# Products of the MLPs' downward weights taken in pairs, by seven block products of half the size

## The chip, the cores and the metric

The kernel runs on one core of a Trainium2 chip. The metric is device time in microseconds (us) of one execution, median of several.

## The reference, cut to what matters

One step of a trunk of two layers on 544 columns (512 new tokens and 8 x 4 sampled ones), width 1024. Each layer is a token mixer (SSD in the first, HGRN in the second) and an MLP, which is what the change is in:

```
h = h + out.astype(h.dtype)
h = h + squared_relu_mlp(rmsnorm(h, norm_mlp_w[layer]), mlp_w_up[layer], mlp_w_down[layer]).astype(h.dtype)
...
def squared_relu_mlp(u, w_up, w_down):
    return jnp.square(jax.nn.relu(u @ w_up)) @ w_down
```

`w_up` is 1024 x 4096, `w_down` 4096 x 1024. All is f32; both a weight and an operand are split into a high and a low part, and a product is taken as high x high, high x low and low x high.

## The kernel before

**Units.** Weights arrive by SyncE's queue in units of 128 x 1024 f32 (`raw`, three buffers). A unit has eight blocks of 128 x 128. `split` (L192, L193) makes the high half on ScalarE (a cast, `whi` or `fh`) and the low half on VectorE (a subtraction, `wlo` or `fl`), for 512 columns at a time. A direct product of a unit (`products`, matmul at L320) is 8 blocks x 3 x 2 halves of 272 columns = 48 matmuls into one PSUM tile of two banks (`acc`).

**Groups.** Each MLP has four groups, q=0 to 3, of 8 units upward and 8 downward. The units of the first MLP are 56 to 119, so q=1 has the ups 72 to 79 and the downs 80 to 87. An up unit gives 128 rows of the hidden layer, which are squared and split into `gh` and `gl` (`g_tiles`, L1012); a down unit multiplies the eight `g` of its group, and the sum is added to the residual `x` (`add_to_x`, L410, 544 columns).

**Pairs.** The ups of q=1 to 3 are taken two at a time by a scheme of seven products. The pair of units and the operand make 2 x 2 blocks, and seven products p1, p2, n6, q7, n5, p3, q4 of sums of blocks take the place of eight: `seventh` (matmul at L1038, 12 matmuls each). The sums of the weights come by DMA and VectorE: `v` is loaded in two halves by SyncE's queue, and GpSimd's queue then adds two more to it in flight; `s2` is one sum, rebuilt in place between n6 and q7 (L245, L249); `a22` is the last block. The sums of the operand are made once per MLP (`operands`). The products share three banks (a, b of `pp`, and `pc`), and between them values are copied out: `s1` after p1, `sv` after n6, `sw` after n5 (L1047, ScalarE); VectorE adds or subtracts them (L1051, L1053, L1055), ScalarE does the relu (L1057, L1059, L1063).

**What sets the order.** `_mlp_plan` writes the list of products: in the pairs by the slots

```
SLOTS = (("p1", 0), ("p2", 1), ("n6", 3), ("q7", 4), ("n5", 6), ("p3", 9), ("q4", 12))
```

at 7 i + t for pair i, so that p3 and q4 of a pair stand among the next pair's products. The first two downs of a group are cut in pieces around the last products of its pairs, and the last down of a group around the first products of the next. `take` makes the weight halves ahead of a product (`conv_unit`, `form`), and loads ahead of these (`load_next`). A scheduler then sets the order of each engine's queue; what stands under `tc.high_priority()` goes forward in it. Each engine runs its queue in order. Halves of sevenths have rings of five of their own, `v` has three buffers, `s2` and `a22` two.

**The ends.** In the last group of each MLP, `then` follows an add to x (`pre_norm`: a scaled split and squares for the next norm). The last two downs of the second MLP are computed by `finish` together with the final norm.

Of the kernel before, what the change touches and what calls it, by code (L numbers as in the profile page):

```python
# [16 lines left out]
P = 128  # L17
# [43 lines left out]
def _mlp_plan(ub):  # L61


    plan = []
    for q in range(MLP_GROUPS):
        b = ub + 16 * q
        if q == 0:
            plan += [("u", b + i) for i in range(8)]
        else:
            slots = sorted((7 * i + t, name, b + 2 * i) for i in range(4) for name, t in SLOTS)  # L70
            slots = [x[1:] for x in slots]
            last = plan.pop()
            piece = lambda k0, k1: last[:2] + (k0, k1) + last[4:]
            plan += [piece(0, 4)] + slots[:2] + [piece(4, 6)] + slots[2:4] + [piece(6, 8)] + slots[4:]
        downs = [("d", b + 8 + m, 0, 8, m, q) for m in range(KT)]
        if q:
            cut = lambda x, k0, k1: x[:2] + (k0, k1) + x[4:]
            tail = plan[-2:]
            plan[-2:] = [cut(downs[0], 0, 4), tail[0], cut(downs[0], 4, 6), tail[1], cut(downs[1], 0, 6), cut(downs[0], 6, 8), cut(downs[1], 6, 8)]
            downs = downs[2:]  # L80
        plan += downs
    return plan
# [14 lines left out]
def trunk(ctx: ExitStack, tc: tile.TileContext, io):  # L97
# [44 lines left out]
    def plan_mlp(ub):  # L142
        plan = _mlp_plan(ub)
        for x in plan:
            if x[0] in "ud":
                if x[0] == "u" or x[2] == 0:
                    loads.append(("u", x[1]))
                    jobs.append((("u", x[1]), len(loads) - 1))
            else:
                if x[0] == "p1":  # L150
                    loads.extend([("v", x[1]), ("u", x[1])])
                if x[0] == "q4":
                    loads.append(("a22", x[1]))
                jobs.append((x, len(loads) - 1))
        return plan

    plans = [plan_mlp(U_MLP)]
# [3 lines left out]
    plans.append(plan_mlp(U_MLP2))  # L161
# [4 lines left out]
    def load_next():  # L166
        kind, u = loads[state["load"]]
        state["load"] += 1
        if kind == "u":
            raw = wraw.tile([P, 1024], F32, tag="raw", name=f"raw{u}")  # L170
            nc.sync.dma_start(raw, io["W"][u])
        elif kind == "a22":
            raw = mp["w"].tile([P, 512], F32, tag="a22", bufs=2, name=f"a22_{u}")
            nc.sync.dma_start(raw, io["W"][u + 1][:, 512:])
        else:

            raw = mp["w"].tile([P, 1024], F32, tag="v", bufs=3, name=f"v{u}")
# [61 lines left out]
    def form(name, u):  # L239
# [3 lines left out]
        if name == "n6":  # L243
            s2 = mp["w"].tile([P, 512], F32, tag="s2", bufs=2, name=f"s2_{u}")
# [708 lines left out]
    def mlp(name, plan, v0, then, last=False):  # L953
        es = ExitStack()
        pool = es.enter_context(tc.tile_pool(name=f"{name}_pool", bufs=4, reuse_waits="tile"))
        gp = es.enter_context(tc.tile_pool(name=f"{name}_g", bufs=9, reuse_waits="tile"))
        ws = es.enter_context(ExitStack())
        mp["w"] = ws.enter_context(tc.tile_pool(name=f"{name}_w", bufs=2, reuse_waits="tile"))
        res = []
        fops = {}  # L960

        sums = []

        def operands():
# [4 lines left out]
            for k in range(4):  # L969
# [14 lines left out]
                t12, t34 = (mp["w"].tile([P, T], F32, tag=f"f{c}", bufs=5, name=f"{name}_t{c}{k}") for c in "hl")  # L984
# [39 lines left out]

        def seventh(name_, u):

            if name_ == "p1":
# [7 lines left out]
            for k in range(4):  # L1035
                oh, ol = fops[name_, k]
# [5 lines left out]
            tick()  # L1042
            keep = {"p1": "s1", "n6": "sv", "n5": "sw"}.get(name_)
            with tc.high_priority():
                if keep:
                    d[keep] = pool.tile([P, HF], F32, tag=keep, bufs=1 + (keep == "sv"), name=f"{keep}_{u}")
                    nc.scalar.copy(d[keep], ps)  # L1047
                if name_ in ("p1", "n6"):
# [20 lines left out]
        for x_ in plan:  # L1069
            if x_[0] == "u":  # L1070
                held.append((x_[1], up(x_[1])))
                if len(held) == 2 or res:
# [6 lines left out]
            elif x_[0] == "d":  # L1079
                _, u, k0, k1, m, q = x_  # L1080
                if k0 == 0:
# [399 lines left out]
def _layout(inp):  # L1481
# [38 lines left out]
    units += mlp(1)  # L1520
# [58 lines left out]
```

## Time and profile before

| | |
|---|---|
| median of 3 runs | 1560.85 us (1560.81 to 1562.58) |
| the profiled execution | 1563.88 us |
| its span | 1562.1 us |
| mean granted TensorE clock | 0.992 |
| matmuls | 13420 |
| first MLP, second MLP | about 465 to 840 us and 1171 to 1548 us |

The span is the profiled part of that execution; a row is read as time, duration, engine, line and tiles, where a tile's buffer numbers are left out (`fh_p` is the high half of the weights of p1, p2 or p3, `fh_n` of n5 or n6, `fh_q` of q4 or q7). PE is TensorE's matmuls, PEld its weight loads, DVE VectorE, ACT ScalarE, POOL GpSimd, SP SyncE.

### The profile page before, as it was taken

How to read it: one execution, taken by the hardware profiler on the slowest of the kernel's cores; microseconds unless marked ns; L12 is line 12 of the kernel's file. 1: busy time of each engine (PE TensorE's matmuls, PEld its weight loads, DVE VectorE, ACT ScalarE, POOL GpSimd, SP SyncE). 2: the span in 40 equal slices, each digit the busy share in tenths (PEclk: the TensorE clock that was granted, in tenths of full speed). 3: DMA queues.
4: the chain of work that ended last, by engine and by line, in shares of the span. 5: the costliest groups of instructions: out<-in, count | busy, mean ns of one | idle time of the engine just before them, and what ended most of it. 6: DMA issues, size and time to landing. Idle time of an engine off the chain costs nothing.

```text
span 1562.1 us, 32717 instructions
## 1 busy us (share of the span) xinstructions
PE 1540.7 (99%) x13420; PEld 1478.1 (95%) x13420; DVE 1092.5 (70%) x2142; ACT 769.4 (49%) x1506; POOL 119.9 (8%) x195
## 2 busy tenths in 40 slices
PE   8999999999999999999999999999999999999997
PEld 7998989898999999999999999999999999999996
DVE  7889798969778555464655788888877555474544
ACT  5684757666355445273654333333344446273552
POOL 3211111110010000010000000000001001010001
PEclk9999999999999999999999999999999999999998
DMA  6466556473545245363323223333235245363311
GB/s 193 111 189 174 144 157 184 110 227 103 149 120 144 88 122 150 95 176 108 84 68 108 78 84 86 109 97 98 74 109 161 89 121 142 108 172 97 97 55 58
DMA packets 87926, 188.94 MB, mean 121 GB/s; under 512 B 14496, under 2 KB 34880, under 8 KB 87776
## 3 DMA queue, kind: packets, MB, share of 16 engines
q1 hardware_dynamic: 74704, 164.21, 33.4%
q0 software_dynamic: 11808, 21.50, 8.7%
q8 instruction: 105, 1.72, 0.4%
q10 hardware_dynamic: 1264, 1.14, 0.2%
q14 instruction: 45, 0.37, 0.1%
HBM read 169.64 MB, written 17.18 MB: 120 GB/s over the span
## 4 chain that ended last, share of the span: by engine, by line
PE 95%; DVE 2%; DMA 1%; issue 1%; ACT 0%; POOL 0%; SPq 0%; POOLq 0%; ACTq 0%
PE ps L320 28%; PE pd L320 24%; PE pp L1038 11%; PE po L320 6%; PE pm L320 6%; PE pc L1038 5%; PE pho L320 3%; PE pa L1177 1%; PE py L624 1%; PE pu L615 1%; PE pi L636 1%; DMA raw<-in_W 1%; PE pn L767 1%; PE pS L1280 1%; PE po L1303 1%
## 5 line engine op out<-in xcount | busy, mean ns | idle before, releaser
L192 ACT CAST whi<-raw 128x512 fp32r<-128x512 f32 x318 | 195.3, 619 | 402.1 <-PE ps L320 156.2
L193 DVE TENSOR_TENSOR wlo<-raw,whi 128x512 fp32r<-128x512 f32 x318 | 218.2, 688 | 94.1 <-ACT whi L192 92.1
L320 PE MATMUL pd<-gh,whi 128*128 128x272 f32 x992 | 205.9, 288 | 0.0
L320 PE MATMUL pd<-gl,whi 128*128 128x272 f32 x992 | 205.4, 288 | 0.0
L320 PE MATMUL pd<-gh,wlo 128*128 128x272 f32 x992 | 205.1, 288 | 0.0
L320 PEld LDWEIGHTS pd<-gh,whi 128*128 128x128 f32 x992 | 156.0, 188 | 0.0
L320 PEld LDWEIGHTS pd<-gh,wlo 128*128 128x128 f32 x992 | 155.7, 188 | 0.0
L320 PEld LDWEIGHTS pd<-gl,whi 128*128 128x128 f32 x992 | 155.5, 188 | 0.0
L320 PE MATMUL ps<-uh_s,whi 128*128 128x272 f32 x576 | 125.6, 300 | 2.5 <-DVE BC L501 2.4
L320 PE MATMUL ps<-ul_s,whi 128*128 128x272 f32 x576 | 121.1, 292 | 0.0
L320 PE MATMUL ps<-uh,whi 128*128 128x272 f32 x512 | 112.7, 300 | 0.0
L320 PE MATMUL ps<-ul,whi 128*128 128x272 f32 x512 | 106.5, 289 | 0.0
L320 PE MATMUL ps<-uh,wlo 128*128 128x272 f32 x512 | 106.2, 289 | 0.0
L410 DVE TENSOR_TENSOR x<-pd,x 128x544 f32<-128x544 f32 x62 | 44.8, 722 | 86.9 <-PE pd L320 86.9
L320 PEld LDWEIGHTS ps<-uh_s,whi 128*128 128x128 f32 x576 | 91.9, 192 | 8.5 <-issue 6.9
L320 PEld LDWEIGHTS ps<-ul_s,whi 128*128 128x128 f32 x576 | 92.0, 191 | 0.3
L181 POOL DMA_DIRECT2D v<-in_W x48 | 42.1, 1028 | 603.8 <-DMA v<-in_W 397.4
L320 PE MATMUL ps<-uh_s,wlo 128*128 128x272 f32 x576 | 85.7, 289 | 0.0
L320 PEld LDWEIGHTS ps<-uh,whi 128*128 128x128 f32 x512 | 80.8, 189 | 3.7 <-issue 1.4
L320 PEld LDWEIGHTS ps<-ul,whi 128*128 128x128 f32 x512 | 80.4, 188 | 0.0
L320 PEld LDWEIGHTS ps<-uh,wlo 128*128 128x128 f32 x512 | 80.1, 188 | 0.0
L320 PEld LDWEIGHTS ps<-uh_s,wlo 128*128 128x128 f32 x576 | 77.4, 188 | 1.1 <-issue 0.8
(428 smaller groups left out, 3811.4 us busy)
## 6 DMA issues: line engine op xcount, KB each, us to landing
raw<-in_W SPq DMA_DIRECT2D x198, 512.0 KB, 3.6
v<-in_W SPq DMA_DIRECT2D x48, 256.0 KB, 4.2
v<-in_W POOLq DMA_DIRECT2D x48, 256.0 KB, 5.8
wlo<-in_W POOLq DMA_DIRECT2D x34, 256.0 KB, 5.7
w<-cum_d SPq DMA_DIRECT2D x16, 512.0 KB, 6.9
st<-in_ssm_in SPq DMA_DIRECT2D x16, 512.0 KB, 4.9
out_ssm_s<-st SPq DMA_DIRECT2D x16, 512.0 KB, 6.8
a<-in_W SPq DMA_DIRECT2D x24, 256.0 KB, 4.3
```

The costliest lines, as they stand in the source:

```text
L181: nc.gpsimd.dma_start(raw[:, c : c + 512], io["W"][u + 1][:, :512], accum_op=ADD)
L192: nc.scalar.copy(hi, raw)
L193: (eng or nc.vector).tensor_tensor(lo, raw, hi.bitcast(F32), SUB)
L320: nc.tensor.matmul(ps[:, h, :HF], block(a, c0 + k * step), o[:, h * HF : (h + 1) * HF], start=(first and i == 0), stop=(last and i == len( ...
L410: nc.vector.tensor_tensor(v3(x[m]), ps[:, :, :HF], v3(x[m]), ADD)
L615: nc.tensor.matmul(pu, bt[:, c], xts[c].rearrange("p h q -> p (h q)"), start=True, stop=True)
L624: nc.tensor.matmul(py[64 * (h % 2) : 64 * (h % 2) + 64, (h // 2) * P : (h // 2 + 1) * P], xds[c][:, h], ws_[c][:, h], start=True, stop=True,)
L636: nc.tensor.matmul(pi[:, j * P : (j + 1) * P], hT[:, j * P : (j + 1) * P], CT[:, cs], start=True, stop=True)
L767: nc.tensor.matmul(pn, bm[:, s], xq.rearrange("p h q -> p (h q)"), start=True, stop=True)
L1038: nc.tensor.matmul(ps, block(w, k * P), o, start=(name_ in ("p1", "p2", "q7") and k == 0 and j == 0), stop=(k == 3 and j == 2), skip_group ...
L1177: nc.tensor.matmul(pv4[b * NS : (b + 1) * NS, c], K[:, bs], QQ[:, 2 - n :, bs], start=True, stop=True, tile_position=(0, b * NS),)
L1280: nc.tensor.matmul(pS[:, c * P : (c + 1) * P], kt[:, c], vt[:, c], start=True, stop=True)
```

## The change

The downs m=2 to 7 of the groups q=1, 2 and 3 are taken by the seven products too, as three pairs a group; in the last group of the second MLP it is m=2 to 5, and m=6 and 7 stay with `finish`. The pairs of downs of a group stand in one list of slots with the next group's pairs of ups. m=0 and m=1 stay direct, cut in pieces as before. For these pairs, sums of the squares' blocks are needed: `square_forms` makes them for each pair of ups with four instructions of 272 columns in the place of the squares themselves (L1052 to L1055) and splits them (two more high and low halves of 544 columns, `m0_gh72_0` and the like). A product of a pair of downs goes into x by itself: three copies (`s1`, `sv`, `sw`, now L1091) and seven adds of 272 columns (L1097 from a copy, L1100 from PSUM) in place of two of 544 (now L424). To make room, `v` goes to two buffers, `s2` and `a22` to one, `g` to eight, and the halves of sevenths share the ring of four of the direct units (`whi`, `wlo`), counted by `state["live"]`. The host lays the columns of these downs out in pairs.

```diff
 MLP_GROUPS = 4
-def _mlp_plan(ub):
+def _mlp_plan(ub, last):
     plan = []
+    pairs = []
+    part = lambda x, k0, k1: x[:2] + (k0, k1) + x[4:]
+    def slots():
+        found = sorted((7 * i + t, name, u) for i, u in enumerate(pairs) for name, t in SLOTS)
+        return [x[1:] for x in found]
     for q in range(MLP_GROUPS):
         b = ub + 16 * q
+        downs = [("d", b + 8 + m, 0, 8, m, q) for m in range(KT)]
         if q == 0:
-            plan += [("u", b + i) for i in range(8)]
-        else:
-            slots = sorted((7 * i + t, name, b + 2 * i) for i in range(4) for name, t in SLOTS)
-            slots = [x[1:] for x in slots]
-            last = plan.pop()
-            piece = lambda k0, k1: last[:2] + (k0, k1) + last[4:]
-            plan += [piece(0, 4)] + slots[:2] + [piece(4, 6)] + slots[2:4] + [piece(6, 8)] + slots[4:]
-        downs = [("d", b + 8 + m, 0, 8, m, q) for m in range(KT)]
-        if q:
-            cut = lambda x, k0, k1: x[:2] + (k0, k1) + x[4:]
-            tail = plan[-2:]
-            plan[-2:] = [cut(downs[0], 0, 4), tail[0], cut(downs[0], 4, 6), tail[1], cut(downs[1], 0, 6), cut(downs[0], 6, 8), cut(downs[1], 6, 8)]
-            downs = downs[2:]
-        plan += downs
+            plan += [("u", b + i) for i in range(8)] + downs
+            continue
+        pairs += [b + 2 * i for i in range(4)]
+        new = slots()
+        if q == 1:
+            d = plan.pop()
+            new = [part(d, 0, 4)] + new[:2] + [part(d, 4, 6)] + new[2:4] + [part(d, 6, 8)] + new[4:]
+        plan += new[:-2] + [part(downs[0], 0, 4), new[-2], part(downs[0], 4, 6), new[-1]]
+        plan += [part(downs[1], 0, 6), part(downs[0], 6, 8), part(downs[1], 6, 8)]
+        whole = last and q == MLP_GROUPS - 1
+        pairs = [b + 8 + m for m in range(2, KT - 2 if whole else KT, 2)]
+        if q == MLP_GROUPS - 1:
+            plan += slots() + (downs[-2:] if whole else [])
     return plan
...
-            raw = mp["w"].tile([P, 512], F32, tag="a22", bufs=2, name=f"a22_{u}")
+            raw = mp["w"].tile([P, 512], F32, tag="a22", bufs=1, name=f"a22_{u}")
             nc.sync.dma_start(raw, io["W"][u + 1][:, 512:])
         else:
-            raw = mp["w"].tile([P, 1024], F32, tag="v", bufs=3, name=f"v{u}")
+            raw = mp["w"].tile([P, 1024], F32, tag="v", bufs=2, name=f"v{u}")
...
         a1 = loaded["u", u]
         v = loaded.get(("v", u))
         if name == "n6":
-            s2 = mp["w"].tile([P, 512], F32, tag="s2", bufs=2, name=f"s2_{u}")
+            s2 = mp["w"].tile([P, 512], F32, tag="s2", bufs=1, name=f"s2_{u}")
             nc.vector.tensor_tensor(s2, v[:, :512], a1[:, :512], ADD)
             loaded["s2", u] = s2
...
             "p1": lambda: a1[:, :512], "p2": lambda: a1[:, 512:], "n6": lambda: s2, "q7": lambda: v[:, 512:],
             "n5": lambda: v[:, :512], "p3": lambda: loaded["s2", u], "q4": lambda: loaded["a22", u],
         }[name]()
-        hi = mp["w"].tile([P, 512], F32R, tag="fh", bufs=5, name=f"fh{u}_{name}")
-        lo = mp["w"].tile([P, 512], F32R, tag="fl", bufs=5, name=f"fl{u}_{name}")
+        hi = wcv.tile([P, 512], F32R, tag="whi", name=f"fh{u}_{name}")
+        lo = wcv.tile([P, 512], F32R, tag="wlo", name=f"fl{u}_{name}")
         split(raw, hi, lo)
         return [hi], [lo]
+    def halves_of(job):
+        return 2 if job[0][0] == "u" else 1
+    def ahead():
+        while state["conv"] < len(jobs) and state["live"] + halves_of(jobs[state["conv"]]) <= 4:
+            state["live"] += halves_of(jobs[state["conv"]])
+            conv_unit()
     def take(key):
         i = place[key]
-        ahead = 0.0
-        j = i
-        while j + 1 < len(jobs) and ahead < 1.0:
-            j += 1
-            ahead += 1.0 if jobs[j][0][0] == "u" else 0.25
-        while state["conv"] <= j:
-            if jobs[state["conv"]][0][0] != "u" and not mp:
-                break
-            conv_unit()
+        if mp:
+            ahead()
+            assert state["conv"] > i
+        else:
+            while state["conv"] <= min(i + 1, len(jobs) - 1) and jobs[state["conv"]][0][0] == "u":
+                conv_unit()
         return ready.pop(key)
     def unit(u):
...
     def mlp(name, plan, v0, then, last=False):
         es = ExitStack()
         pool = es.enter_context(tc.tile_pool(name=f"{name}_pool", bufs=4, reuse_waits="tile"))
-        gp = es.enter_context(tc.tile_pool(name=f"{name}_g", bufs=9, reuse_waits="tile"))
+        gp = es.enter_context(tc.tile_pool(name=f"{name}_g", bufs=8, reuse_waits="tile"))
         ws = es.enter_context(ExitStack())
+        tp = ws.enter_context(tc.tile_pool(name=f"{name}_t", bufs=8, reuse_waits="tile"))
         mp["w"] = ws.enter_context(tc.tile_pool(name=f"{name}_w", bufs=2, reuse_waits="tile"))
+        state["live"] = 2 * len(ready)
         res = []
         fops = {}
+        gops = {}
+        first = plan[0][1]
         sums = []
...
-                t12, t34 = (mp["w"].tile([P, T], F32, tag=f"f{c}", bufs=5, name=f"{name}_t{c}{k}") for c in "hl")
+                t12, t34 = (tp.tile([P, T], F32, tag=f"t{c}", name=f"{name}_t{c}{k}") for c in "hl")
...
         banks = {}
+        def square_forms(u, a0, a1):
+            k = (u - first) % 16 // 2
+            (h0, l0), (h1, l1) = g[u], g[u + 1]
+            gops["p1", k] = h0[:, :HF], l0[:, :HF]
+            gops["p2", k] = h1[:, :HF], l1[:, :HF]
+            gops["p3", k] = h1[:, HF:], l1[:, HF:]
+            b11, b12, b21, b22 = a0[:, :HF], a0[:, HF:], a1[:, :HF], a1[:, HF:]
+            nc.vector.tensor_tensor(b11, b11, b12, SUB)
+            nc.vector.tensor_tensor(b12, b12, b22, SUB)
+            nc.vector.scalar_tensor_tensor(b22, b11, -1.0, b22, MUL, SUB)
+            nc.vector.tensor_tensor(b21, b21, b22, ADD)
+            for i, (t, n1, n2) in enumerate(((a1, "q4", "n6"), (a0, "n5", "q7"))):
+                th, tl = (tp.tile([P, T], F32R, tag=f"t{c}", name=f"{name}_g{c}{u}_{i}") for c in "hl")
+                split(t, th, tl)
+                gops[n1, k] = th[:, :HF], tl[:, :HF]
+                gops[n2, k] = th[:, HF:], tl[:, HF:]
+        def release(n):
+            state["live"] -= n
         def seventh(name_, u):
+            q, r = divmod(u - first, 16)
+            down = r >= 8
+            ops_ = gops if down else fops
             if name_ == "p1":
                 ac = acc_tile(f"pp{u}")
                 banks[u] = d = {"a": ac[:, 0, :HF], "b": ac[:, 1, :HF]}
...
             ps = d[{"p2": "b", "q7": "c", "q4": "c"}.get(name_, "a")]
             hi, lo = take((name_, u))
             for k in range(4):
-                oh, ol = fops[name_, k]
+                oh, ol = ops_[name_, k]
                 for j, (w, o) in enumerate(((hi, oh), (hi, ol), (lo, oh))):
                     nc.tensor.matmul(
                         ps, block(w, k * P), o, start=(name_ in ("p1", "p2", "q7") and k == 0 and j == 0),
                         stop=(k == 3 and j == 2), skip_group_check=name_ in ("n6", "n5", "p3", "q4"),
                     )
             tick()
+            release(1)
             keep = {"p1": "s1", "n6": "sv", "n5": "sw"}.get(name_)
-            with tc.high_priority():
-                if keep:
+            if keep:
+                with tc.high_priority():
                     d[keep] = pool.tile([P, HF], F32, tag=keep, bufs=1 + (keep == "sv"), name=f"{keep}_{u}")
                     nc.scalar.copy(d[keep], ps)
+            if down:
+                m = r - 8
+                x1, x2 = ([x[i][:, :HF], x[i][:, HF:]] for i in (m, m + 1))
+                at = {"p1": x1[0], "p2": x1[0], "p3": x1[1], "n6": x2[0], "q4": x2[0], "n5": x2[1], "q7": x2[1]}[name_]
+                if keep:
+                    nc.vector.tensor_tensor(at, at, d[keep], ADD if name_ == "p1" else SUB)
+                else:
+                    with tc.high_priority():
+                        nc.vector.tensor_tensor(at, ps, at, ADD)
+                if q == MLP_GROUPS - 1 and name_ in ("p3", "q4"):
+                    then(m + (name_ == "q4"))
+                return
+            with tc.high_priority():
                 if name_ in ("p1", "n6"):
                     d[name_] = pool.tile([P, T], F32, tag="a", name=f"a{u}_{name_}")
                 if name_ == "p2":
...
             if name_ == "q4":
                 nc.scalar.activation(d["n6"], d["n6"], AF.Relu)
                 g_tiles(u + 1, d["n6"])
+                square_forms(u, d["p1"], d["n6"])
         g = {}
         acc = {}
...
         for x_ in plan:
             if x_[0] == "u":
                 held.append((x_[1], up(x_[1])))
+                release(2)
                 if len(held) == 2 or res:
                     if not res:
                         while not res:
...
                         finish([unit(u - 1), unit(u)], ops, [acc[KT - 2][0], acc[m][0]])
                         continue
                     acc[m][1] = unit(u)
+                else:
+                    ahead()
                 ps, w = acc[m]
                 gb = u - 8 - m
                 products(ps, w, [g[gb + k] for k in range(k0, k1)], k0 == 0, k1 == 8, k0 * P)
+                release((k0 < 4 <= k1) + (k1 == 8))
                 if k1 == 8:
                     add_to_x(m, ps, then if q == MLP_GROUPS - 1 else None)
             else:
...
-    def mlp(l):
+    def mlp(l, last):
...
+            ms = slice(2, 2 if q == 0 else KT - 2 if last and q == MLP_GROUPS - 1 else KT)
+            d[ms] = d[ms].reshape(-1, P, KT // 2, 2, P).transpose(0, 1, 3, 2, 4).reshape(-1, P, 1024)
...
```

Three places in the queues, each in the first MLP's second group (q=1). A name's last number is the tile's own; `gh`, `gl` are halves of squares, `a` the squares and before them the values, `m0_g...` the halves of the sums of squares.

ScalarE, around the copy `sv_76` of the third pair, before:

```order
L192 CAST fh76_n5_7165<-v76_6867 128x512
L192 CAST fh78_p1_7191<-raw78_7042 128x512
L1057 ACTIVATE a74_p1_6994<-pp74_6974 128x272
L1059 ACTIVATE a76_p1_7144<-a76_p1_7144 128x272
L1012 ACTIVATE a74_p1_6994<-a74_p1_6994 128x544
L1047 COPY sv_76_7207<-pp76_7124 128x272
L192 CAST gh74_7183<-a74_p1_6994 128x544
L192 CAST fh78_p2_7211<-raw78_7042 128x512
L192 CAST fh76_p3_7227<-s2_76_7103 128x512
```

and after:

```order
L200 CAST fh76_n5_7198<-v76_6912 128x512
L200 CAST gh74_7194<-a74_p1_6992 128x544
L1116 ACTIVATE a76_p1_7154<-a76_p1_7154 128x272
L200 CAST fh78_p1_7222<-raw78_7061 128x512
L200 CAST fh78_p2_7238<-raw78_7061 128x512
L1091 COPY sv_76_7214<-pp76_7133 128x272
L200 CAST fh76_p3_7273<-s2_76_7134 128x512
L1120 ACTIVATE a74_n6_7054<-a74_n6_7054 128x544
L1030 ACTIVATE a74_n6_7054<-a74_n6_7054 128x544
L1091 COPY sw_76_7289<-pp76_7133 128x272
```

`gh74` and the cast `fh78_p2` of the next pair's second product stood behind `sv_76`; now they stand ahead of it.

VectorE, from the low half `fl76_n6` of the third pair to `gl74`, before:

```order
L193 TENSOR_TENSOR fl76_n6_7106<-s2_76_7103,fh76_n6_7105 128x512
L245 TENSOR_TENSOR s2_78_7250<-v78_7037,raw78_7042 128x512
L249 TENSOR_TENSOR s2_76_7103<-s2_76_7103,raw76_6872 128x512
L1053 TENSOR_TENSOR a74_n6_7062<-pc74_7063,sw_74_7121 128x272
L193 TENSOR_TENSOR fl76_q7_7127<-v76_6867,fh76_q7_7126 128x512
L193 TENSOR_TENSOR gl73_7100<-a72_n6_6922,gh73_7099 128x544
L193 TENSOR_TENSOR wlo81_1_7422<-raw81_7292,whi81_1_7420 128x512
L193 TENSOR_TENSOR fl74_q4_7148<-a22_74_6995,fh74_q4_7147 128x512
L1051 TENSOR_TENSOR a76_p1_7144<-pp76_7124,s1_76_7142 128x272
L193 TENSOR_TENSOR fl76_n5_7166<-v76_6867,fh76_n5_7165 128x512
L193 TENSOR_TENSOR fl78_p1_7192<-raw78_7042,fh78_p1_7191 128x512
L193 TENSOR_TENSOR gl74_7184<-a74_p1_6994,gh74_7183 128x544
```

and after:

```order
L201 TENSOR_TENSOR fl76_n6_7137<-s2_76_7134,fh76_n6_7136 128x512
L1054 SCALAR_TENSOR_TENSOR a72_n6_6910<-a72_p1_6860,a72_n6_6910 128x272
L257 TENSOR_TENSOR s2_76_7134<-s2_76_7134,raw76_6917 128x512
L1055 TENSOR_TENSOR a72_n6_6910<-a72_n6_6910 128x272
L201 TENSOR_TENSOR fl76_q7_7157<-v76_6912,fh76_q7_7156 128x512
L201 TENSOR_TENSOR fl74_q4_7177<-a22_74_7012,fh74_q4_7176 128x512
L201 TENSOR_TENSOR m0_gl72_0_7107<-a72_n6_6910,m0_gh72_0_7106 128x544
L201 TENSOR_TENSOR m0_gl72_1_7111<-a72_p1_6860,m0_gh72_1_7110 128x544
L1108 TENSOR_TENSOR a76_p1_7154<-pp76_7133,s1_76_7152 128x272
L201 TENSOR_TENSOR fl76_n5_7199<-v76_6912,fh76_n5_7198 128x512
L201 TENSOR_TENSOR gl74_7195<-a74_p1_6992,gh74_7194 128x544
L1052 TENSOR_TENSOR a74_p1_6992<-a74_p1_6992 128x272
```

The last two forms of pair 72, two low halves of its sums (`m0_gl72_0`, `m0_gl72_1`) and the first form of pair 74 have come in; the sum `s2_78` and the low half of direct unit 81 have gone to a later place.

VectorE at the first downs of the group behind the direct ones, before:

```order
L193 TENSOR_TENSOR gl79_7497<-a78_n6_7358,gh79_7496 128x544
L193 TENSOR_TENSOR wlo82_1_7506<-raw82_7334,whi82_1_7504 128x512
L410 TENSOR_TENSOR x_75<-pd1_0_7406,x_75 128x544
L193 TENSOR_TENSOR wlo83_0_7578<-raw83_7411,whi83_0_7576 128x512
L410 TENSOR_TENSOR x_75<-pd1_1_7500,x_75 128x544
L193 TENSOR_TENSOR wlo83_1_7579<-raw83_7411,whi83_1_7577 128x512
L193 TENSOR_TENSOR wlo84_0_7638<-raw84_7417,whi84_0_7636 128x512
L410 TENSOR_TENSOR x_75<-pd1_2_7573,x_75 128x544
```

and after:

```order
L1055 TENSOR_TENSOR a78_n6_7375<-a78_n6_7375 128x272
L201 TENSOR_TENSOR m0_gl78_0_7550<-a78_n6_7375,m0_gh78_0_7549 128x544
L201 TENSOR_TENSOR m0_gl78_1_7554<-a78_p1_7313,m0_gh78_1_7553 128x544
L424 TENSOR_TENSOR x_75<-pd1_0_7452,x_75 128x544
L201 TENSOR_TENSOR fl82_n6_7622<-s2_82_7619,fh82_n6_7621 128x512
L424 TENSOR_TENSOR x_75<-pd1_1_7557,x_75 128x544
L257 TENSOR_TENSOR s2_82_7619<-s2_82_7619,raw82_7453 128x512
L201 TENSOR_TENSOR fl82_q7_7641<-v82_7389,fh82_q7_7640 128x512
L201 TENSOR_TENSOR fl82_n5_7660<-v82_7389,fh82_n5_7659 128x512
L1097 TENSOR_TENSOR x_75<-x_75,s1_82_7656 128x272
L1100 TENSOR_TENSOR x_75<-pp82_7638,x_75 128x272
```

Where the adds of `pd1_0` to `pd1_2` stood between low halves of direct units, the last form, its low halves, two adds, the sum `s2_82` and the low halves of pair 82 follow one another, and the adds of its products into x begin.

More of the change, by code (lines that the diff above doesn't have):

```diff
@@ L140, in trunk, with plan_mlp @@
     jobs = [(("u", u), u) for u in range(U_MLP)]
-    def plan_mlp(ub):
-        plan = _mlp_plan(ub)
+    def plan_mlp(ub, last):
+        plan = _mlp_plan(ub, last)
         for x in plan:
@@ L155, in plan_mlp @@
         return plan
-    plans = [plan_mlp(U_MLP)]
+    plans = [plan_mlp(U_MLP, False)]
     for u in range(U_HGRN_IN, U_MLP2):
@@ L160, in trunk @@
         jobs.append((("u", u), len(loads) - 1))
-    plans.append(plan_mlp(U_MLP2))
+    plans.append(plan_mlp(U_MLP2, True))
     place = {key: i for i, (key, _) in enumerate(jobs)}
@@ L1508, in _layout @@
             units.append(out4(wo[512 * g : 512 * (g + 1)])[j : j + 1])
-    def mlp(l):
+    def mlp(l, last):
         w1, w2 = up(f["mlp_w_up"][l]), f["mlp_w_down"][l]
-        return [t for q in range(MLP_GROUPS) for t in (w1[8 * q : 8 * q + 8], down(w2[1024 * q : 1024 * (q + 1)]))]
-    units += mlp(0)
+        ts = []
+        for q in range(MLP_GROUPS):
+            d = down(w2[1024 * q : 1024 * (q + 1)]).copy()
+            ms = slice(2, 2 if q == 0 else KT - 2 if last and q == MLP_GROUPS - 1 else KT)
+            d[ms] = d[ms].reshape(-1, P, KT // 2, 2, P).transpose(0, 1, 3, 2, 4).reshape(-1, P, 1024)
+            ts += [w1[8 * q : 8 * q + 8], d]
+        return ts
+    units += mlp(0, False)
     hi = up(f["hgrn_w_in"][0])
@@ L1519, in _layout @@
     units += [out4(ho[:512]), out4(ho[512:])]
-    units += mlp(1)
+    units += mlp(1, True)
     a["W"] = np.concatenate(units, axis=0)
```

## The prediction

> **What bounds the kernel now.** First the page: span, busy time and the chain of waits.
>
> ```profile
> span 1562.1 us, 32717 instructions
> PE 1540.7 (99%) x13420; PEld 1478.1 (95%) x13420; DVE 1092.5 (70%) x2142; ACT 769.4 (49%) x1506; POOL 119.9 (8%) x195
> PE 95%; DVE 2%; DMA 1%; issue 1%; ACT 0%; POOL 0%; SPq 0%; POOLq 0%; ACTq 0%
> ```
>
> TensorE is busy all the time and is 95% of the chain, so a matmul taken away is worth its slot, as long as the engines that feed TensorE keep up. So the two MLPs were read next: the chain in order of time (start, duration, what).
>
> ```profile
> 516.11 45.30 PE pd L320 x360
> 653.55 1.52 PE pp L1038 x12
> 745.64 1.49 PE pp L1038 x12
> ```
>
> The first row gives the price of a matmul of 272 columns: 45.30 / 360 = **0.1258 us**. Twelve (one half-size product) are 1.51 us, a pair of downs in 96 is 12.08, in 84 it is 10.57. The other two rows are the same place of groups q=2 and q=3: one group lasts 92.09 us. It has 4 x 84 + 8 x 48 = 720 matmuls, 90.58 us, so **1.5 us of a group are lost, 0.37 per pair**. The table by stage says where (columns: PE, PEld, DVE, ACT, POOL busy with counts, clock, DMA share, GB/s):
>
> ```profile
> 653.00:697.00 44.00, 43.93 (x340) 42.65 (x339) 29.12 (x48) 28.85 (x58) 4.48 (x6) 1.00 0.54 146
> 697.00:745.50 48.50, 48.50 (x388) 48.50 (x388) 20.60 (x32) 15.24 (x27) 2.51 (x3) 1.00 0.43 108
> ```
>
> The loss is in the up pairs (first row: weight loads 42.65 of 44); the direct downs (second row) lose nothing, with VectorE and ScalarE at less than half. The clock is 1.00 in both. What TensorE waits for in the pairs, from its waits in the first MLP and two of its gaps:
>
> ```profile
> PEld pp L1038 <- ACT s L1047: 2.1, 9, 0.3
> PEld pp L1038 <- DVE a_p L1051: 1.3, 6, 0.3
> 655.93 0.19 PEld L1038 LDWEIGHTS pp<-m_b2h,fh_p 128*128 128x128 f32 x1 [0.20 <-ACT s L1047]
> 658.31 0.19 PEld L1038 LDWEIGHTS pp<-m_th,fh_n 128*128 128x128 f32 x1 [0.20 <-DVE a_p L1051]
> ```
>
> These are the hand-overs of the scheme itself: p2 adds into its bank only after the copy of p1 (s1), n6 only after p2 is read out.
>
> **The change, part by part.** *Matmuls.* 9 pairs of downs in the first MLP and 8 in the second go from 96 to 84: 17 x 12 = 204 fewer, 204 x 0.1258 = **-25.7 us**. Everything else is what this is paid with. The prices of VectorE and ScalarE, from their rows beside the pairs:
>
> ```profile
> 672.70 0.73 DVE L193 TENSOR_TENSOR gl<-a_p,gh 128x544 fp32r<-128x544 f32 x1
> 673.34 0.68 DVE L193 TENSOR_TENSOR fl_p<-s,fh_p 128x512 fp32r<-128x512 f32 x1
> 673.94 0.69 DVE L193 TENSOR_TENSOR wlo<-raw,whi 128x512 fp32r<-128x512 f32 x1
> 674.54 0.43 DVE L1055 TENSOR_TENSOR a_n<-pc,sv 128x272 f32<-128x272 f32 x1
> 674.89 0.68 DVE L193 TENSOR_TENSOR fl_n<-s,fh_n 128x512 fp32r<-128x512 f32 x1
> ```
>
> ```profile
> 671.74 0.38 ACT L1047 COPY sv<-pp 128x272 f32<-128x272 f32 x1
> 672.01 0.65 ACT L192 CAST gh<-a_p 128x544 fp32r<-128x544 f32 x1
> 672.60 0.62 ACT L192 CAST fh_p<-s 128x512 fp32r<-128x512 f32 x1
> 673.12 1.13 ACT L192 CAST whi<-raw 128x512 fp32r<-128x512 f32 x2
> ```
>
> By the starts, one after the other without a gap, VectorE takes 0.64 for 544 columns, 0.60 for 512, 0.35 for 272; ScalarE 0.59, 0.52 and 0.27. An **up pair** now needs on VectorE 7 low halves and 2 sums of weights (512), 2 low halves of its squares, 2 of the new forms (544), 3 adds that empty PSUM and 4 forms (272): 9 x 0.60 + 4 x 0.64 + 7 x 0.35 = **10.4 us of TensorE's 10.57** (before: 7.7). ScalarE has about 9.3 (7 x 0.52, 4 x 0.59, 3 x 0.27 and about 2.4 of relu and squares). A **down pair** has 9 x 0.60 + 7 x 0.35 = 7.9 on VectorE, 7 x 0.52 + 3 x 0.27 = 4.5 on ScalarE. Loads are therefore covered in both, in up pairs with almost no margin. What remains are waits in queues that run in order. I walked the new order of each engine through the second group with these durations; what I get is an estimate:
>
> - *Steady down pair:* the same two hand-overs (s1 copy, p2 read out). Row 0.37 per pair of the trace; the walk gives 0.32, since ScalarE has less in its queue: 17 x 0.32 = **+5.4**.
> - *Up pairs beside the forms.* The first two of a group stay at 0.37. In the third (u=76) gh74 and fh78_p2 now stand ahead of the copy sv_76 that n5_76 waits for; fh78_p2 waits for n6_76 to end, as only four halves are alive. Cast 0.52 and copy 0.38 are 0.90 with nothing for hand-overs, and only 7 matmuls (0.88) stand on TensorE between n6 and n5. The walk: 0.57 there, 0.24 at s1, 0.28 where a76_p1 stands behind two low halves of the forms, 0.14 more: 1.23. The fourth (u=78) has the same before sv_78, behind whi80: 0.86. Together 1.23 + 0.86 - 2 x 0.37 = 1.35 a group, six groups: **+8.1**. Bounds: 0 if these queues have drained, and, if the first two pairs of a group get 1.23 too, 2 x 0.86 x 6 = 10.3 more.
> - *Switch from ups to down pairs.* The adds of pd_0 and pd_1 stand on VectorE behind the forms of the last pair, and fl82_n6, the second sum s2_82 and fl82_q7 behind or between them. TensorE's p1_82 waits for the first add (its bank), 0.13; the third matmul of q7_82 for fl82_q7: 0.84; n6: 0.15. 1.12 x 6 = **+6.7**. Bounds 0 and, if the whole stretch of add, sum and two low halves (0.64 + 0.60 + 2 x 0.60 = 2.44) is open, 14.6.
> - *Ends.* Two last down pairs without successors wait for sw: 0.3 each, **+0.6**.
>
> Edits at nothing: the adds into x.
>
> ```profile
> L410 DVE TENSOR_TENSOR x<-pd,x 128x544 f32<-128x544 f32 x62 | 44.8, 722 | 86.9 <-PE pd L320 86.9
> ```
>
> Two of these per pair go and seven of 272 come; VectorE sat idle 86.9 us ahead of them, and they are within the 7.9 above. The last group of an MLP adds the next norm's scaled low halves and squares, up to 2.7 us per pair: 10.5 of 10.57, covered, with nothing left (one open us per pair would be 5 in all). The smaller rings:
>
> ```profile
> v<-in_W SPq DMA_DIRECT2D x48, 256.0 KB, 4.2
> v<-in_W POOLq DMA_DIRECT2D x48, 256.0 KB, 5.8
> ```
>
> ```profile
> 439.38 1.99 DVE L193 TENSOR_TENSOR yl<-zs,yh 128x544 fp32r<-128x544 f32 x3
> 446.73 0.60 ACT L213 CAST whi<-raw 128x512 fp32r<-128x512 f32 x1
> ```
>
> With two v tiles, a tile is rewritten after its n5 half is made and needed by the sum before n6 of the second pair after: 11 products, 16.6 us, against 4.2 + 5.8 = 10.0 and some 2 of POOL's issue. Covered by 4 us. A later one would stop VectorE's queue at the sum, and TensorE's n6 behind it, for as long: 41 us if each of the 24 + 17 pairs came 1 us beyond the cover, and I take 0. A down pair loads 512 + 4 x 256 + 256 KB in 11 us, 163 GB/s, where a stretch of direct downs has 108 (row 697); the up pairs' stretch (row 653) carries 146 and TensorE waits for no v there. POOL issues 82 additions in place of 48 and is idle otherwise. On SP's queue the loads of v72, v74 and a22_72 now stand ahead of raw57. They need tiles of the SSD, last read by yl until 441.4; raw57 needs the cast that ends at 447.33. Nothing is late. The weights' pool shares its four halves with the direct units, at worst another late cast, which is in the walk.
>
> **Sum:** -25.7 + 5.4 + 8.1 + 6.7 + 0.6 = **-4.9 us**. The profiled execution took 1563.88 (span 1562.1 and 1.8 around it); it is 0.2% above the median of 1560.85. 1563.88 - 4.9 = 1559.0, at the median **1556.0**.
>
> **The rivals.** (B) *VectorE and ScalarE catch up.* ScalarE's idle time in the stretch 655 to 697 is a wait for TensorE, which speaks for slack in its queue:
>
> ```profile
> L192 ACT CAST fh_p<-raw 128x512 fp32r<-128x512 f32 x6 | 3.7, 621 | 11.9 <-PE pp L1038 11.8
> ```
>
> Then every pair loses 0.37 only and the switch nothing: -25.7 + 17 x 0.37 = -19.4: **1541.5**. Against it: a queue in order that is 98% full catches up with nothing.
>
> (C) *VectorE becomes the bound of the up pairs: slower.* Its waits for TensorE and its dependent steps cannot be filled:
>
> ```profile
> L1051 DVE TENSOR_TENSOR a_p<-pp,s 128x272 f32<-128x272 f32 x4 | 1.8, 440 | 2.3 <-PE pp L1038 2.3
> L1055 DVE TENSOR_TENSOR a_n<-pc,sv 128x272 f32<-128x272 f32 x3 | 1.3, 439 | 1.0 <-PE pc L1038 0.9
> 499.65 0.43 DVE L987 SCALAR_TENSOR_TENSOR m_th<-m_th,m_n 128x272 f32<-128x272 f32 x1
> 500.12 0.44 DVE L989 TENSOR_TENSOR m_tl<-m_n,m_th 128x272 f32<-128x272 f32 x1
> ```
>
> Per pair that is 2.3 / 4 + 1.0 / 3 = 0.91 of waits, and 0.47 in place of 0.35 for each of four forms that need the one before, 0.48. 10.41 + 0.91 + 0.48 = 11.80 in place of 10.94: 0.86 x 24 up pairs = +20.6, over -25.7 + 5.4 + 6.7 + 0.6 = -13.0: +7.6, **1568.5**. It decides from 10.94 + 13.0 / 24 = 11.48 us per up pair on. For it: the forms have to be done before the group's downs, so they cannot be put off. Against it: the two direct downs of a group (96 matmuls, 12.1 us) give VectorE a stretch with little load, and the last forms may wait until then.
>
> (D) *Each VectorE instruction waits for the end of the one before.* By the durations in place of the starts an up pair has 9 x 0.69 + 4 x 0.73 + 7 x 0.44 = 12.2 us: 1.27 x 24 = +30.5 - 13.0 = +17.5, **1578**. The rows 673.34, 673.94 and 674.54 speak against it: 0.60 apart, while each lasts 0.68. The Trainium skill, VectorE: DVE Perf Modes, section The DRAIN you can't avoid, has this rule: the next operation does not start until the pipe is empty, though one that is not held starts earlier. The rows side with the exception here; where forms depend on one another, as at 499.65, they side with the rule.
>
> That the change does not do what it says is settled by the count of matmuls: 13216.
>
> **How the numbers follow.** The walk as it stands 0.50; its own range, with the 20.8 of stalls 30% off either way, is 1550 to 1562. B 0.23, C 0.21, D 0.06. The range 1541 to 1568 leaves out D, half of C, and a little of B: 0.2. About 0.2% (3.1 us) is what a measurement of this kernel can tell, that is 1557.7 and 1564.0. Faster: 0.35 of the walk and B: 0.58. Same: 0.13 of the walk, 0.03 of C: 0.16. Slower: the rest, 0.26.
>
> **What would show it.** Matmuls 13216, each still 0.126. First p1 of a group to the next: 91.0 us by the walk (684 matmuls 86.1, stalls 4.9); 88.7 under B; 93.1 (4 x 11.80 + 3 x 10.89 + 12.08 + 1.12) under C, with VectorE busy without gaps in up pairs. TensorE's waits: sv and a_p in the third and fourth up pair, a low half of q7 at each switch. If waits for raw or v appear, or forms (L1052 to L1055) end later than the direct pieces of the downs, I am wrong on the rings or on the switch. I'd be wrong throughout if the down pairs lost more than 1 us each: 17 x 0.7 = 12, and the gain is gone.

## The result and the profile after

| kernel | median, us | runs | ratio to before (95%) |
|---|---|---|---|
| before | 1560.84 | 4 (1560.81 to 1562.58) | |
| with the change | 1550.22 | 4 (1548.48 to 1550.77) | 0.9927 (0.9910 to 0.9944) |

The change makes the kernel 10.6 us faster, 0.7%. The forecast was 4.8 us: the right sign and half the size.

The page of the kernel after, span, busy time and chain:

```profile
span 1546.7 us, 33087 instructions
PE 1522.2 (98%) x13216; PEld 1450.3 (94%) x13216; DVE 1233.1 (80%) x2456; ACT 841.3 (54%) x1656; POOL 150.4 (10%) x229
PE 6%; DVE 1%; issue 1%; POOL 0%; ACT 0%; POOLq 0%; DVEq 0%
```

There are 13216 matmuls, 204 fewer. VectorE has 140 us more to do. The chain is followed only over the last 8% here, so the stages have to be read from tiles. First and last start of one tile's matmuls, of the kernel before, then after: `pm` begins the first MLP, `pa` the HGRN, `pS` ends it, and `fn_pc` begins the final norm.

```profile
L320 PE MATMUL pm<-uh,whi x256: 286/288/376, 465.5 to 1221.0; 128*128 128x272 f32 x128
L1177 PE MATMUL pa<-q,K x1280: 196/196/243, 859.4 to 1118.2; 128*32 128x32 f32 x146, 128*32 128x64 f32 x37
L1280 PE MATMUL pS<-vt,kt x64: 272/275/377, 890.6 to 1133.4; 128*128 128x128 f32 x64
L1418 PE MATMUL fn_pc<-ones,ssq x12: 166/219/219, 1540.1 to 1549.9; 128*91 128x1 f32 x12
```

```profile
L334 PE MATMUL pm<-uh,whi x256: 286/288/376, 461.1 to 1211.7; 128*128 128x272 f32 x128
L1239 PE MATMUL pa<-q,K x1280: 196/196/243, 849.9 to 1108.7; 128*32 128x32 f32 x146, 128*32 128x64 f32 x37
L1342 PE MATMUL pS<-vt,kt x64: 272/275/377, 881.1 to 1123.9; 128*128 128x128 f32 x64
L1480 PE MATMUL fn_pc<-ones,ssq x12: 164/219/219, 1525.8 to 1535.6; 128*91 128x1 f32 x12
```

The first MLP takes 388.8 us in place of 393.9, the stretch with the second 401.9 in place of 406.7: **-5.1 and -4.8, -9.9 in all**. The HGRN (pa to pS) takes 274.0 in both. The two profiled spans differ by more, 15.4 us, because the SSD stage, which the change does not touch, is 4.4 us shorter in the second, and the part from `fn_pc` on 1.1 us (20.9 in place of 22.0). Two stretches of the SSD stage, before and after (PE, PEld, DVE, ACT and POOL busy, clock, DMA share, GB/s):

```profile
120.00:180.00 60.00, 56.58 (x427) 52.69 (x427) 50.64 (x92) 31.99 (x67) 7.81 (x15) 0.94 0.60 165
420.00:465.50 45.50, 43.69 (x319) 42.36 (x319) 32.42 (x58) 22.54 (x38) 1.92 (x3) 0.92 0.42 117
```

```profile
120.00:180.00 60.00, 56.58 (x439) 52.67 (x438) 50.35 (x92) 33.21 (x70) 7.83 (x15) 0.97 0.61 169
420.00:461.10 41.10, 39.21 (x305) 37.95 (x304) 30.43 (x56) 20.73 (x36) 5.22 (x6) 1.00 0.58 159
```

The granted clock was 0.92 in the last 45 us of that stage before, and 1.00 after (0.92 of 45.5 us is 41.9). That belongs to one execution and not to the change: in the profiles of the other kernels with the change (below), the first MLP begins between 461.2 and 464.7 us. The medians differ by 10.6.

What TensorE waits for in the pairs, whole run (engine, tile, line, waited for: us, times, longest), before and then after:

```profile
PEld pp L1038 <- ACT s L1047: 4.3, 18, 0.3
PEld pp L1038 <- DVE a_p L1051: 2.6, 12, 0.3
```

```profile
PEld pp L1081 <- ACT s L1091: 5.0, 18, 0.8
PEld pp L1081 <- ACT sv L1091: 3.9, 18, 0.2
PEld pp L1081 <- DVE a_p L1108: 3.7, 18, 0.5
PEld pc L1081 <- DVE fl_q L201: 3.1, 5, 0.6
PEld pp L1081 <- DVE x L424: 1.4, 6, 0.3
PEld pp L1081 <- ACT sw L1091: 1.3, 2, 0.8
```

6.9 us have become 18.4. This view misses a part of what a wait costs (the last section has the row), so below the waits are counted from the starts of neighbouring matmuls: what lies beyond the slot of 0.1258 us, where it is over 0.05, for the products of the pairs in both MLPs, by the pair in its group and the product that starts late.

```
us lost, 6 groups         before  after   per pair after   forecast per pair
up pair 1 (p2, n6)          3.01   3.52       0.59             0.37
up pair 2 (p2, n6)          3.54   3.23       0.54             0.37
up pair 3 (p2, n6, n5, q4)  2.77   4.75       0.79             1.23
up pair 4 (p2, n5)          1.01   2.23       0.37             0.86
first down pair                -   9.51       1.59             1.12 + 0.32
second and third (11)          -   3.31       0.30             0.32, ends 0.6
sum                        10.33  26.55
```

So -25.7 + (26.55 - 10.33 = 16.2) = **-9.5 us**, which the stages' -9.9 and the medians' -10.6 agree with. The change gives back 63% of what it takes away from TensorE. From the first p1 of a group to the next the kernel before takes 92.1 us and the kernel after 90.0 to 90.4; the prediction had asked for 91.0 by the walk, 88.7 under B and 93.1 under C.

The busiest place is where the forms are made. After, the third up pair, the fourth with the first direct pieces, then a first down pair and a second one:

```profile
578.30:589.40 11.10, 11.10 (x86) 10.59 (x85) 10.89 (x21) 9.16 (x20) 1.76 (x2) 1.00 0.69 168
589.40:604.50 15.10, 15.10 (x119) 14.73 (x118) 14.48 (x27) 12.74 (x25) 3.51 (x4) 1.00 0.64 165
706.00:717.30 11.30, 10.90 (x81) 10.15 (x79) 8.11 (x16) 4.93 (x11) 1.79 (x2) 1.00 0.46 116
717.30:728.30 11.00, 10.95 (x87) 10.73 (x86) 9.49 (x18) 5.69 (x11) 1.76 (x2) 1.00 0.66 165
```

VectorE is busy 10.89 of 11.10 us in the third up pair and 96% in the next stretch, yet of these four stretches TensorE loses most in the row at 706, a first down pair, where VectorE is busy 8.11 of 11.30.

### The profile page after: what moved, and what is told of

It is laid out like the page before. It is cut to its first block, busy times and chain, and to the rows that moved or that the text cites. A ratio compares the mean times of both kernels' runs of the same rounds, so it can differ in the third digit from the quotient of the medians.

```text
span 1546.7 us, 33087 instructions
## 1 busy us (share of the span) xinstructions
PE 1522.2 (98%) x13216; PEld 1450.3 (94%) x13216; DVE 1233.1 (80%) x2456; ACT 841.3 (54%) x1656; POOL 150.4 (10%) x229
## 5 line engine op out<-in xcount | busy, mean ns | idle before, releaser
L200 ACT CAST whi<-raw 128x512 fp32r<-128x512 f32 x250 | 154.1, 618 | 298.4 <-PE ps L334 153.7
L201 DVE TENSOR_TENSOR wlo<-raw,whi 128x512 fp32r<-128x512 f32 x250 | 171.6, 689 | 56.5 <-ACT whi L200 54.6
L189 POOL DMA_DIRECT2D v<-in_W x82 | 72.0, 1036 | 687.2 <-DMA v<-in_W 432.4
L334 PE MATMUL pd<-gh,whi 128*128 128x272 f32 x448 | 94.1, 289 | 0.0
L334 PE MATMUL pd<-gl,whi 128*128 128x272 f32 x448 | 92.6, 288 | 0.0
L334 PE MATMUL pd<-gh,wlo 128*128 128x272 f32 x448 | 92.0, 286 | 0.0
L201 DVE TENSOR_TENSOR fl_p<-raw,fh_p 128x512 fp32r<-128x512 f32 x82 | 55.8, 689 | 29.9 <-ACT fh_p L200 27.4
L200 ACT CAST fh_p<-raw 128x512 fp32r<-128x512 f32 x82 | 50.5, 620 | 52.0 <-PE pp L1081 16.2
L334 PEld LDWEIGHTS pd<-gh,whi 128*128 128x128 f32 x448 | 70.6, 188 | 0.0
L334 PEld LDWEIGHTS pd<-gl,whi 128*128 128x128 f32 x448 | 70.5, 188 | 0.0
```

The costliest lines, as they stand in the source:

```text
L200: nc.scalar.copy(hi, raw)
L201: (eng or nc.vector).tensor_tensor(lo, raw, hi.bitcast(F32), SUB)
L334: nc.tensor.matmul(ps[:, h, :HF], block(a, c0 + k * step), o[:, h * HF : (h + 1) * HF], start=(first and i == 0), stop=(last and i == len( ...
```

## The experiments

Three readings of the 16.2 us were open: single waits, made by the order of the queues (the theory of the prediction); VectorE as the bound of the up pairs (rival C); and the hand-overs, which the prediction called those "of the scheme itself". Each kernel is timed beside the kernel before. The 95% interval of a ratio is 1.3 to 1.8 thousandths either way, 2.0 to 2.8 us, so differences of one to three us between kernels with the change are read from the waits counted in their traces; by the medians alone they are not shown.

### The second sum made later

At the switch, VectorE's rows (start, duration) and TensorE's late row after them are, in the kernel after:

```profile
615.36 0.72 DVE L424 TENSOR_TENSOR x<-pd,x 128x544 f32<-128x544 f32 x1
616.00 0.68 DVE L201 TENSOR_TENSOR fl_n<-s,fh_n 128x512 fp32r<-128x512 f32 x1
616.60 0.71 DVE L424 TENSOR_TENSOR x<-pd,x 128x544 f32<-128x544 f32 x1
617.23 0.68 DVE L257 TENSOR_TENSOR s<-s,raw 128x512 f32<-128x512 f32 x1
617.83 0.68 DVE L201 TENSOR_TENSOR fl_q<-v,fh_q 128x512 fp32r<-128x512 f32 x1
```

```profile
618.56 0.19 PEld L1081 LDWEIGHTS pc<-m_gh,fl_q 128*128 128x128 f32 x1 [0.62 <-DVE fl_q L201]
```

The low half of q7 ends at 618.51 behind two adds into x and the sum s2, and q7's matmul starts 0.05 later. The edit takes the sum from ahead of it:

```diff
-        if name == "q7":
+        if name == "p3":
             s2 = loaded["s2", u]
             nc.vector.tensor_tensor(s2, s2, a1[:, 512:], ADD)
```

> The change, with the second sum s2 made when p3's weights are (in place of q7's), so that the low half of q7 stands behind one add less on VectorE. Theory (waits come from the order of VectorE's queue at single places): q7's third matmul no longer waits 0.55 us at each of the six switches to the down pairs, and the 0.1 behind it goes too: 6 x 0.55 = 3.3 us less than the changed kernel, about 1547 us, and the rows of the switch lose the wait for fl_q. Rival (VectorE is full there, what leaves one place comes back at the next): within 0.7 us of the changed kernel, 1550.

1548.79 us, ratio 0.9918 (0.9901 to 0.9936). In the counted waits of first down pairs, q7 went from 2.92 to 0.38 us and p2 behind it from 1.61 to 0.77, as expected. But p3 went from 0.80 to 3.00 and the next pair's p1 from 0 to 1.03. All waits of the pairs are 1.6 us fewer, and the median is 1.4 us below the change's, between the theory's 3.3 and the rival's 0.7. The wait is made where it was said to be made; taking it away brought another one, now for the copy sw:

```profile
PEld pp L1081 <- ACT sw L1091: 3.5, 6, 0.8
```

### The copy sv ahead of the cast, and both edits

In the third pair (ScalarE, then TensorE, of the kernel after):

```profile
587.55 0.62 ACT L200 CAST fh_p<-raw 128x512 fp32r<-128x512 f32 x1 [0.39 <-PE pp L1081]
588.08 0.38 ACT L1091 COPY sv<-pp 128x272 f32<-128x272 f32 x1
```

```profile
587.36 0.29 PE L1081 MATMUL pp<-m_th,fl_n 128*128 128x272 f32 x1
588.51 0.19 PEld L1081 LDWEIGHTS pp<-m_th,fh_n 128*128 128x128 f32 x1 [0.22 <-ACT sv L1091]
```

The row at 587.36 is n6's last matmul. This is the wait the prediction described, cast, copy, n5; the row shows 0.22, and counted it is 0.27 per third pair, not 0.57. The edit issues the second cast after sv behind it (the weights of a direct unit likewise):

```diff
-        split(raw, hi, lo)
+        if "sv" in state and state["conv"] > state["sv"][1] + 1:
+            with tc.issue_after(state["sv"][0].ins):
+                split(raw, hi, lo)
+        else:
+            split(raw, hi, lo)
...
-                    nc.scalar.copy(d[keep], ps)
+                    copied = nc.scalar.copy(d[keep], ps)
+                if keep == "sv":
+                    state["sv"] = (copied, state["conv"])
```

> The change, with the cast that stood ahead of the copy sv on ScalarE issued behind it. Theory (n5 of the third and fourth up pair waits 0.25 us each because sv stands behind a cast): 12 waits go, 3.0 us less than the changed kernel, about 1547 us, no wait for sv at n5 of pairs 76 and 78. Rival (ScalarE's queue is pressed, the cast is then late and TensorE waits for a weight half instead): within 0.7 us of the changed kernel, 1550.

1547.41 us, ratio 0.9910 (0.9892 to 0.9928). n5 of the third pair loses 0.64 in place of 1.60 us, n5 of the fourth 1.46 in place of 1.59: there sv itself now starts only when n6 has ended, and too few matmuls stand between. All waits of the pairs are 2.3 us fewer and the median is 2.8 us lower, near the 3.0 expected, but the waits for sv are not gone as the theory said.

> Both edits together (second sum at p3, cast behind sv). Theory: they are at different places and on different engines, so they add: 6.3 us less than the changed kernel, about 1544. Rival: no gain, or that of one alone.

1545.71 us, ratio 0.9895 (0.9878 to 0.9911); waits of the pairs 3.1 us fewer than with the change alone. The two do not add up to 6.3: by the waits half of it, by the medians 4.5 us. Places in a queue can be mended one at a time, and part of what leaves one comes back at another.

### More and less work for VectorE

```diff
                 split(t, th, tl)
+                if i == 0:
+                    nc.vector.tensor_tensor(tl, t, th.bitcast(F32), SUB)
```

> The change, with one of the two new low halves of 544 columns computed twice in each up pair: 0.64 us more on VectorE in each of 24 pairs, nothing else. Theory (single waits, VectorE not the bound): at most 3 us more than the changed kernel, at the switches and where p2's add stands behind the low halves. Rival (VectorE is the bound of the third and fourth up pair): 0.64 x 12 = 7.7 us more, about 1558.

1553.99 us, ratio 0.9947 (0.9931 to 0.9962), against 0.9927: 3 us more by the ratios, 3.8 by the medians, and 4.2 us more of waits, for 24 x 0.64 = 15.4 us of work. That is the theory's 3 or a little over it, and half of the rival's 7.7. The opposite:

```diff
-                split(t, th, tl)
+                nc.scalar.copy(th, t)
+                tl = th
```

> The change, with the low halves of the sums of squares not computed (the high halves are used in their place, so two subtractions of 544 columns are left out in each of 24 up pairs, 1.28 us of VectorE each). Theory (single waits): what stands behind them gains, p2 and n6 of the third pair and p1 at the switch, 2 to 4 us less than the changed kernel, about 1547. Rival (VectorE is the bound of the third and fourth pair): 1.28 x 12 = 15 us less, as far as waits are there to be taken away; at least 8.

1545.37 us, ratio 0.9892 (0.9876 to 0.9907): 5.5 us less of waits for 30.7 us of VectorE's work left out. This is between the two expectations (at most 4 and at least 8), nearer to the theory's. VectorE's load counts where something waits behind it and nowhere else; a bound would have given more.

### The second bank in a tile of its own

p2 writes bank b, while the copy s1 reads bank a; n6 writes a, while VectorE reads p2's result from b. Neither needs the other. But a and b are the two banks of one tile `pp`, and p2's row waits for s1 and n6's for the read-out of p2 (`s` and `a_p` in the list of waits above). The edit gives b a tile from the ring that also holds `pc`, and leaves the second bank of `pp` empty, on the change and on the kernel before alike:

```diff
-                banks[u] = d = {"a": ac[:, 0, :HF], "b": ac[:, 1, :HF]}
+                banks[u] = d = {"a": ac[:, 0, :HF], "b": mx(f"pb{u}")[:, :HF]}
```

> The change, with the second bank (b, written by p2 alone) in a PSUM tile of its own instead of the second half of the two-bank tile pp. Theory: p2's wait for the copy s1 and n6's wait for the read-out of p2 are between different banks and exist only because both banks are one tile; then the waits at p2 and n6 (8.8 + 6.2 = 15.0 us in the changed kernel) nearly go: 12 to 15 us less, about 1537. Rival (VectorE and ScalarE are so full that TensorE then waits elsewhere, for weight halves or sv): half of it, about 1543, with new waits for fh, fl or sv.

> The kernel before with the same one edit: bank b in a tile of its own. Theory: its pairs lose 10.3 us at p2 and n6 and nothing else, so 10 us less than before, about 1551, which is what the change brings by itself. Rival: as above, half.

With the change 1524.47 us, ratio 0.9764 (0.9750 to 0.9777), **25.7 us less than the change alone where 12 to 15 were expected**. The kernel before with it 1551.21, ratio 0.9936 (0.9923 to 0.9948), 10 us less, as expected: of its 10.33 us of counted waits none is left. All that is left of TensorE's waits in the pairs, with the change:

```profile
PEld pp L1081 <- ACT sw L1091: 0.6, 1, 0.6
PEld pc L1081 <- DVE fl_q L201: 0.6, 2, 0.3
```

Up pairs lose nothing, down pairs 2.1 us in all, and the waits for sv and for q7's low half went too, which the edit does not touch. The order of the queues says why. The matmuls on TensorE at the first down pair, as runs of one product, with the change and with the edit:

```
pp82 p1 x12, pc82 q7 x3, pp82 p2 x12, pc82 q7 x5, pp82 n6 x12, pc82 q7 x4, pp84 p1 x3, pp82 n5 x12
pp82 p1 x12, pb82 p2 x12, pp82 n6 x12, pc82 q7 x12, pp82 n5 x12
```

With the wait, the scheduler's order has three matmuls of q7 between p1 and p2, and q7's third matmul is the first that needs its low half. Without the wait q7 stands 24 matmuls after p1, 3.0 us, and VectorE's queue, where the two adds, the sum and the low half of q7 keep their order, is in time. On ScalarE, sv_76 now stands ahead of gh74 and of the cast fh78_p2. VectorE is as busy as before, in the third pair:

```profile
577.60:588.20 10.60, 10.60 (x87) 10.60 (x86) 10.48 (x21) 9.01 (x19) 1.64 (x2) 1.00 0.71 174
```

10.48 of 10.60 us, and TensorE has no gap. Of the 26.5 us of counted waits 2.1 are left. 15.0 of them stood at p2 and n6 themselves and went with the shared tile; the other 9.4 stood at q7, n5, p1, p3 and q4, and that the new order took these away is read from the rows, not tested by a run of its own.

> The change with bank b apart, the second sum at p3 and the cast behind sv. Theory: the three act at different places; 15 + 5 us less than the changed kernel, about 1531. Rival: VectorE is at its bound by then, no better than bank b apart alone.

1524.91 us, ratio 0.9765 (0.9751 to 0.9778): no better than bank b apart alone. The rival's time came out, but not for its reason, since almost nothing is left there to take away (2.0 us of waits in the pairs). The next run puts the reason itself to the test.

> The change with bank b apart, and one of the two new low halves of each up pair computed twice (0.64 us more on VectorE in each of 24 pairs). With bank b apart VectorE is busy 10.48 of 10.60 us in the third pair of a group and TensorE waits for nothing. Theory (VectorE is close to its bound only there, and what it cannot do goes on into the direct downs behind): 0 to 4 us more than with bank b apart alone, 1524.5 to 1528.5. Rival (VectorE is the bound of third and fourth pairs by now): 0.5 to 0.64 us in each of 12 pairs, 6 to 8 us more, about 1531.

1524.29 us, ratio 0.9762 (0.9749 to 0.9776): nothing more. The third pair and the stretch behind it:

```profile
578.00:588.60 10.60, 10.60 (x87) 10.60 (x86) 10.57 (x21) 8.88 (x19) 1.13 (x2) 1.00 0.63 140
588.60:603.80 15.20, 15.20 (x123) 15.20 (x123) 15.13 (x31) 12.60 (x26) 3.52 (x4) 1.00 0.71 189
```

VectorE is busy to the last tenth for 25 us and TensorE waits for none of it: what is not urgent is put off into the direct downs. Rival C is out: VectorE bounds neither the changed kernel, where 15.4 us of added work cost 3 to 4, nor this one, where they cost nothing.

Of these kernels, the change with bank b apart is the fastest that computes only what is needed: 36.8 us less than before. Against the kernel before with the same edit, the change is worth 1551.21 - 1524.47 = 26.7 us. By the two MLP stages of the traces it is 24.7, which is 25.7 us of matmuls less some waits, as far as these measurements can tell.

## Why the prediction was half right

- *Matmuls, -25.7:* right, 204 fewer, each 0.1258 us.
- *Down pairs, 5.4 + 6.7 + 0.6 = 12.7:* measured 9.51 + 3.31 = 12.8. The split is close too: 1.59 for the pair at the switch against 1.44, 0.30 for the others (ends included) against 0.37 (5.4 + 0.6 less the six first pairs' 1.9, over 11). The low half of q7 behind adds and sum was right to the instruction. Inside the switch the agreement is partly luck: q7 lost 0.49 and not 0.84, p1 0.28 and not 0.13, and n5, which the prediction had at nothing, 0.26.
- *Up pairs beside the forms, +8.1:* this is the mis-sized term. Its mechanism, cast ahead of sv, is in the rows, but n5 loses 0.27 (1.60 / 6) and not 0.57, and the fourth pair loses 0.37 and not 0.86. Measured +3.4 in all. With 0.90 of cast and copy against 0.88 of matmuls, 0.57 leaves 0.55 for hand-overs and for a ScalarE that is late. In the rows of the third pair it is 0.24: the cast starts 0.19 after n6's last matmul (587.36 to 587.55), and n5 0.05 after sv ends (588.46 to 588.51). ScalarE was not late there; it stood idle for 0.39 ahead of the cast. That the walk had let small delays of ScalarE add up, and that the waits of TensorE give the queues their time back elsewhere too, is my reading and not tested. This term is all of the 4.6 us by which the sum was off (-4.9 against -9.5).
- *Edits at nothing:* TensorE has no wait for v, raw or a22 in the pairs. VectorE's sum s2 waits for a `raw` twice, 1.7 us in all, where it was twelve times and 9.1 us before. So the two v tiles, the smaller rings and SP's order cost nothing that shows.
- *"These are the hand-overs of the scheme itself":* wrong, and the costliest sentence of the prediction, though its sum does not show it. They belong to a tile that holds two banks. I took 0.37 us per up pair as a price of the method and charged 0.32 to each of 17 new pairs; bank b apart, it is nothing in the kernel before, and with the change the up pairs lose nothing and the first down pairs 1.0 in place of 9.5.
- *Rivals:* B (1541.5) asked for queues that catch up, and named TensorE's old 0.37 as what stays; with the shared tile they do not catch up everywhere, with bank b apart they nearly do, and the 0.37 goes too. C needs up pairs of 11.48 us; by the counted waits they last 10.57 + 13.73 / 24 = 11.14, with VectorE nearly full, and no more than that. D would have needed 12.2 us of VectorE in a pair of 11.1.

## What to carry to other kernels

Before a wait is booked as the price of a method, look at what the waiting instruction writes and what the awaited one reads: if they are different banks of one tile, a tile of its own for each is a one-line edit. Here it was worth 25.7 us on top of the change, which alone brought 10.6, and 10.0 in the kernel before. A wait of a quarter of a microsecond can also go with another order of the queues around it, so waits elsewhere can hang on it. An engine that is 99% busy need not be the bound: VectorE was busy 25.70 of 25.80 us here, and more work on it cost nothing, because the work that TensorE waits for was in time. Adding and removing work is what showed it.

## What the runs showed of the hardware

In these rows a wait of TensorE costs more than the idle time shown. Its matmuls around p2's wait, then the weight load ahead of it, the one that waited and the next, in the kernel after:

```profile
558.83 0.29 PE L334 MATMUL pd<-gh,whi 128*128 128x272 f32 x1
559.11 0.39 PE L1081 MATMUL pp<-m_b2h,fh_p 128*128 128x272 f32 x1
559.34 0.29 PE L1081 MATMUL pp<-m_b2l,fh_p 128*128 128x272 f32 x1
559.47 0.29 PE L1081 MATMUL pp<-m_b2h,fl_p 128*128 128x272 f32 x1
```

```profile
558.71 0.19 PEld L334 LDWEIGHTS pd<-gh,whi 128*128 128x128 f32 x1
559.11 0.19 PEld L1081 LDWEIGHTS pp<-m_b2h,fh_p 128*128 128x128 f32 x1 [0.21 <-ACT s L1091]
559.22 0.19 PEld L1081 LDWEIGHTS pp<-m_b2l,fh_p 128*128 128x128 f32 x1
```

The first matmul comes 0.28 after its forerunner in place of 0.126 and lasts 0.39 in place of 0.29, and the second starts 0.23 behind it, 0.10 late once more. The two delays are 0.15 + 0.10 = 0.26 us (before rounding), where the weight load's row shows 0.21 of idle time. Over all waits of the pairs, taken as the matmuls that last over 0.35, these second delays make 10.6 us in the kernel after (102 waits) and 4.4 before (42). The Trainium skill, TensorE: Matmul & The Clock Gate, section Step-by-step: what each phase is for, says that weight loads are pulled ahead so that the next tile's weights load while this one's matmul runs; the rows agree: the loads at 558.71 and 559.22 start 0.12 us ahead of their matmuls at 558.83 and 559.34, under the matmul before, while the load that waits starts with its own matmul at 559.11.
